# Chunk-sum tables of a state-space block: summing two products by accumulating matmuls instead of an elementwise add

## Chip, cores and metric

The kernel runs on one core of a Trainium2 chip. The metric is the time of one execution on the device, in microseconds (us). TensorE, VectorE, ScalarE, GpSimd and the DMA queues each work through an instruction list of their own, in order; semaphores join them. In the rows, PE is TensorE's matmuls, PEld its weight loads, DVE VectorE, ACT ScalarE, POOL GpSimd.

## The reference

Two transformer-like blocks follow one another on a 512 x 1024 sequence. Only the first block is touched: one layer of latent attention beside a two-directional diagonal state-space mixer.

```python
h = _rms_norm(x, pre_norm_g[l])
z = h @ w_in[l]
z_q, z_kv, z_kr, g_attn, u_ssm, g_ssm = jnp.split(z, split_points, axis=-1)
attn = _mla_attention(z_q, z_kv, z_kr, positions, ...)
...
lam_bar = jnp.exp(lam * dt)
b_bar = ((lam_bar - 1.0) / lam)[..., None] * b
bu = jnp.einsum('sbgh,gph->sbgp', u_c, b_bar)          # complex
_, h = lax.associative_scan(_diag_scan_op, (a, bu), reverse=reverse, axis=0)
y = y + jnp.real(jnp.einsum('sbgp,ghp->sbgh', h, c))
```

There are 32 groups of 16 channels, 64 complex states per group and two directions (2 x 64 = 128 partitions).

## The kernel before

The scan is done in 64 chunks of 8 positions. For each group a table F holds lam_bar to a power (1 to 8) times b_bar, real and imaginary part; F transposed, times the chunk's inputs `U`, is the chunk's sum. A recurrence over the chunks (`recur`, with `step` and the `fx` corrections) then runs on VectorE in the tile `st`.

The 32 groups go in 8 slices of 4. `table` makes a slice's table on VectorE with three passes over 128 x 1024 elements: a product into `tb` (line 457), a product into `ot` (line 457), and their sum into `tb` (line 458). `f_slice` then transposes the table on TensorE, 8 transposes per slice into PSUM tiles `ftr` (line 474); ScalarE copies each bank of four to an SBUF tile `f` (line 476); 8 matmuls of `f` with `U` write `vps` (line 481), each recorded as two passes in the trace; ScalarE copies `vps` to `st` in two halves (line 483). `rounds` staggers the slices: in one round a slice is multiplied, the next one transposed, and the one after that gets its table.

`table` is also used by `prep` for another set of tables (EP, EQ times c): two of these come ahead of the recurrence, six later.

Work around it, on the same engines: the projection to `U`; two gate projections of 96 matmuls each, the first (i = 0) free to run, the second (i = 1) ordered on TensorE behind the last chunk-sum matmul; then the projection `z` and its norm (`zn`, `ztr`, `zl`), the products V and QR made from it, and after these the attention heads, which are interleaved with the remaining tables and the outputs `y_slice`. The order of each engine's list is set when the program is built, from a timeline of estimated durations; the chip then runs each list in order.

Buffers by tag that matter here: "E" 2 (`tb`), "et" 1 (`ot`), "PT" 4 (`f` among others), "Y" 1 (the later `yo`). PSUM banks: two each for "tr", "sc", "o", "mm".

Of the kernel before, what the change touches and what calls it, by code (L numbers as in the profile page):

```python
# [64 lines left out]
class Net:  # L65
# [240 lines left out]
    def block1(self):  # L306

        nc, A, tc = self.nc, self.A, self.tc
        mm = nc.tensor.matmul
# [7 lines left out]
        for o in ORD1.split():  # L317
            n = int(o[1])
# [4 lines left out]
            elif o[0] == "g":  # L323
                g = self.gain("pre_norm_g", 0, tag="E")
# [31 lines left out]
        def feat(wh, wl, m):  # L356
            p = self.ps("mm")
            ms = slice(m * 128, (m + 1) * 128)
            for k in range(8):
                self.mm3(self.tiled(p), wh[k][:, ms], wl[k][:, ms], xh[k], xl[k], k == 0, k == 7)  # L360
            return p

        def tok(wh, wl, t, cw):
            p = self.ps("mm")
            for k in range(8):
                self.mm3(p[:, :cw], xh[k][:, t], xl[k][:, t], wh[k], wl[k], k == 0, k == 7)
            return p[:, :cw]
# [4 lines left out]
        for t in range(NT):  # L372
            p = tok(wh, wl, t, 512).rearrange("p (g h) -> p g h", g=G)
            nc.scalar.copy(yt[:, :, 2 * t], p[0:64])
            nc.scalar.copy(yt[:, :, 2 * t + 1], p[64:128])
        U = self.act(shape=[128, G, 64], name="U", tag="U")
        for q in range(4):
            p = self.ps("tr" if q < 2 else "sc", "utr")
# [47 lines left out]
        br, bi = bB[:, 0], bB[:, 1]  # L426
        braw = [self.act(shape=[128, G, 16], name="braw", tag="S") for _ in range(2)]
        for i in range(2):
# [6 lines left out]
        EP, EQ, FP, FQ = (self.act(shape=[128, G, 2, 8], name=n, tag=t)  # L435
                          for n, t in (("EP", "sq"), ("EQ", "sq"), ("FP", "T"), ("FQ", "T")))
# [11 lines left out]
        nc.scalar.copy(EQ[:, :, 0], EP[:, :, 1])  # L448
        nc.scalar.activation(EQ[:, :, 1], EP[:, :, 0], AF.Copy, scale=-1.0)

        def table(P, Q, xr, xi, s):

            sh = [128, 4, 16, 16]
            o, t = (self.act(shape=sh, name=n, tag=g) for n, g in (("tb", "E"), ("ot", "et")))
            for d, p, x in ((o, P, xr), (t, Q, xi)):
                p = p[:, s * 4:s * 4 + 4].rearrange("p g r e -> p g (r e)")[:, :, :, None].to_broadcast(sh)
                nc.vector.tensor_tensor(d, p, x[:, :, None, :].to_broadcast(sh), OP.mult)
            nc.vector.tensor_tensor(o, o, t, OP.add)
            return o.rearrange("p g (r e) h -> p g r (e h)", r=2)

# [3 lines left out]
        last = [None]  # L464

        def f_slice(s):
            gs = slice(s * 4, s * 4 + 4)
            ft = table(FP, FQ, br[:, gs], bi[:, gs], s)
            yield
            f = []  # L470
            for r in range(2):
                p = self.ps("sc" if s % 2 else "tr", "ftr")
                for gg in range(4):
                    nc.tensor.transpose(p[:, gg * 128:(gg + 1) * 128], ft[:, gg, r], self.ident)
                f.append(self.act(shape=[128, 4, 128], name="f", tag="PT"))
                nc.scalar.copy(f[r].rearrange("p g e -> p (g e)"), p)
            yield
            pv = self.ps("o", "vps").rearrange("p (g r c) -> p g r c", r=2, g=4)
            for r in range(2):
                for gg in range(4):  # L480
                    last[0] = mm(pv[:, gg, r], f[r][:, gg], U[:, s * 4 + gg], start=True, stop=True)
            for ps_, o in ((slice(0, 64), 1), (slice(64, 128), -1)):
                nc.scalar.copy(st[ps_, gs].rearrange("p g r j s -> p (g r) j s"),
                               pv[ps_, :, :, ::o].rearrange("p g r (s j) -> p (g r) j s", j=8))

        rounds((s, f_slice(s)) for s in range(8))


# [47 lines left out]
        def prep(s):  # L536

            gs = slice(s * 4, s * 4 + 4)
            c_ = self.small([128, 2, 4, 16], bufs=2, name="cc")
            for i in range(2):  # L540
                nc.sync.dma_start(c_[:, i], A["s5_c"][i][:, gs])
            e = table(EP, EQ, c_[:, 0], c_[:, 1], s)
            nc.sync.dma_start(Ed[s], e.rearrange("p g r e -> p (g r e)"))
            yield
            bb = bbs[s % 2]
            for d in range(2):
                ps_, cs_ = slice(d * 64, d * 64 + 64), slice(d * 32, d * 32 + 16)
                nc.scalar.copy(bb[ps_, :, :, cs_], bB[ps_, :, gs])
            p = self.ps("sc", "kps")
            for gg in range(4):  # L550
                for r in range(2):
                    mm(p[:48, gg * 128:(gg + 1) * 128], bb[:, r, gg], e[:, gg, r], start=r == 0, stop=r == 1)
            kst = self.act(shape=[128, 4, 8, 16], name="kst", tag="K")
            pv = p.rearrange("p (g t h) -> p g t h", g=4, t=8)
            nc.scalar.copy(kst[0:48], pv[0:48])
            k7 = self.small([16, 4, 16], bufs=1, name="k7")
            nc.scalar.copy(k7, pv[32:48, :, 7])
            dd = self.small([16, 4, 16], bufs=1, name="dd")
            nc.vector.tensor_tensor(dd, Dd[:, gs, None].to_broadcast([16, 4, 16]),
                                    self.ident[0:16, None, 0:16].to_broadcast([16, 4, 16]), OP.mult)  # L560
            nc.vector.tensor_tensor(k7, k7, dd, OP.add)
            nc.vector.tensor_tensor(kst[0:16, :, 0], kst[0:16, :, 0], k7, OP.add)
            kd = Kd[s]
            nc.sync.dma_start(kd[:, :, 112:240], kst[0:16].rearrange("p g t h -> p g (t h)"))
            nc.sync.dma_start(kd[:, :, 0:112], kst[32:48, :, 0:7].rearrange("p g t h -> p g (t h)"))
# [51 lines left out]
        for i in range(2):  # L617
            wh, wl = self.weights([A["w1_in"][1 + i, j] for j in range(4)])
            for m in range(4):
                with ExitStack() as late:  # L620
                    if i:
                        late.enter_context(tc.issue_after(last[0].ins))
                    p = feat(wh, wl, m)
# [49 lines left out]
        for t in range(NT):  # L673
            ts = slice(t * 128, (t + 1) * 128)
            p = self.ps("mm")
            self.mm3(p, Z[0][:, 2, ts], Z[1][:, 2, ts], wk_h[1], wk_l[1], True, True)
            self.split(V[0][:, t], V[1][:, t], p)
        for t in range(NT):
            ts = slice(t * 128, (t + 1) * 128)
            p = self.ps("mm")  # L680
# [3 lines left out]
            pv = p[:, :256].rearrange("p (h f) -> p h f", h=4)  # L684
            pv, qav, qbv = (a.rearrange("p h (a f) -> p h a f", a=2) for a in (pv, qa, qb))
# [6 lines left out]
            p = self.ps("tr", "qtr")  # L692
# [97 lines left out]
        def rnorm(i):  # L790
            p = self.ps("g", "nps")
            for t in range(NT):
                mm(p[:, 2 * t:2 * t + 2], sqa[i][:, t * 128:(t + 1) * 128], ones, start=True, stop=True)
            s_ = self.small([128, NT], name="nss", bufs=2)
            nc.vector.tensor_copy(s_, p[:, 0:8].rearrange("p (t a) -> p t a", a=2)[:, :, 0])
            return self.rowsum(s_, 512)

        y = [self.b8([128, 4, 512], F32, name="y1") for _ in range(2)]
        r = rnorm(0)
        for half in range(2):  # L800
            wh, wl = self.weights([A["w1_out"][half, i] for i in range(2)])
            for t in range(NT):
                p = self.ps("g", "mm")
# [8 lines left out]
        sh, sl = (self.b8([128, 4, 512], name=n) for n in ("sgh", "sgl"))  # L812
# [4 lines left out]
        for m in range(4):  # L817
            p = self.ps("g", "mm")
# [7 lines left out]
            f = self.act(name="gf", tag="c")  # L826
# [3 lines left out]
        r = rnorm(1)  # L830
        mark = self.last_y
        g = self.gain("post_norm_g", 0, mark, "E")
# [5 lines left out]
        for t in range(NT):  # L838
            ss = self.small([128, 2], name="pss")
            gy = []  # L840
            for half in range(2):
                wh, wl = w[half]
                p = self.ps("g", "mm")
# [705 lines left out]
```

## Time and profile before

| | before |
|---|---|
| median of 3 runs | 1656.55 us |
| lowest, highest run | 1652.34, 1658.28 us |
| the profiled execution | 1654.3 us |
| span of its instructions | 1652.0 us |
| granted TensorE clock, mean | 0.983 |
| TensorE busy in the span | 96% |
| VectorE busy in the span | 58% |
| ScalarE busy in the span | 48% |

The profiled execution is 2.25 us below the median; 2.3 us of it lie outside the span. Shares of the whole span are means over the stages of two blocks, so the stretch around the change has to be looked at by itself: the chunk sums stand between 43 and 92 us of the span, the recurrence and the projections behind them up to about 172 us.

### The profile page before, as it was taken

The numbers are of one execution on the slowest core, as the hardware profiler recorded it, in microseconds if no ns is written. First come the engines' busy times: TensorE is split into PE (matmuls) and PEld (weight loads), VectorE is DVE, ScalarE is ACT, GpSimd is POOL, SyncE is SP. The second block draws the span as 40 slices with busy tenths as digits, with TensorE's granted clock in tenths as the row PEclk, the third lists the DMA queues.
The fourth block names the chain that finished last, engine by engine and source line by source line (L and its number), as shares of the span: only waits on it lengthen the run. The fifth ranks groups of instructions, "written<-read, shape, count | busy, mean of one in ns | idle before, by whom it ended". The sixth has DMA issues, their size and how long they took to land.

```text
span 1652.0 us, 22681 instructions
## 1 busy us (share of the span) xinstructions
PE 1591.1 (96%) x8240; PEld 1342.2 (81%) x8240; DVE 952.2 (58%) x1863; ACT 794.7 (48%) x1548; POOL 397.7 (24%) x492
## 2 busy tenths in 40 slices
PE   7997999899999999999999999999999999999998
PEld 5876888688888888888888888888878888888886
DVE  7989665855787865323333465488865632333334
ACT  5734686543677845333232443377774433323242
POOL 2001120413465712101010130355571210101012
PEclk9987999999999999999999999999999999999999
DMA  4222343444222442333333333412233233333332
GB/s 163 85 77 70 110 118 122 160 151 154 54 63 57 116 153 77 97 89 96 102 102 102 103 130 118 149 48 56 58 101 128 64 99 93 102 103 102 102 100 79
DMA packets 71406, 167.43 MB, mean 101 GB/s; under 512 B 14464, under 2 KB 23168, under 8 KB 71296
## 3 DMA queue, kind: packets, MB, share of 16 engines
q1 hardware_dynamic: 70528, 165.21, 32.7%
q8 instruction: 65, 1.06, 0.3%
q10 hardware_dynamic: 768, 0.79, 0.2%
q14 instruction: 45, 0.37, 0.1%
HBM read 145.80 MB, written 10.98 MB: 95 GB/s over the span
## 4 chain that ended last, share of the span: by engine, by line
PE 72%; issue 10%; DVE 9%; ACT 4%; DMA 2%; POOL 2%; ACTq 0%; SPq 0%; DVEq 0%; POOLq 0%
PE mm L177 20%; PE mm L175 20%; PE mm L176 20%; PE ptr L953 2%; DVE sc L928 2%; DVE pt L145 1%; PE cps L1001 1%; PE oacc L963 1%; PE oacc L962 1%; PE sc L927 1%; PE sc L924 1%; DMA ql<-ql 1%; ACT ysq L207 1%; DMA swap<-raw 1%; DVE wlo L145 1%
## 5 line engine op out<-in xcount | busy, mean ns | idle before, releaser
L145 DVE TENSOR_TENSOR wlo<-wst,whi 128x1024 fp32r<-128x1024 f32 (+3 forms) x209 | 254.7, 1223 | 252.9 <-ACT whi L144 249.1
L175 PE MATMUL mm<-xT,whi 128*128 128x512 f32 (+1 forms) x896 | 338.3, 381 | 0.1
L144 ACT CAST whi<-wst 128x1024 fp32r<-128x1024 f32 (+3 forms) x209 | 215.1, 1033 | 253.8 <-PE mm L177 125.1
L176 PE MATMUL mm<-xT,whi 128*128 128x512 f32 (+1 forms) x896 | 335.8, 376 | 0.0
L177 PE MATMUL mm<-xT,wlo 128*128 128x512 f32 (+1 forms) x896 | 326.7, 377 | 0.9 <-DVE wlo L145 0.8
L1389 POOL TENSOR_TENSOR relu<-relu 128x512 f32<-128x512 f32 x64 | 67.0, 1046 | 539.7 <-ACT relu L1388 539.7
L177 PE MATMUL mm<-whi,hl 128*128 128x512 f32 x512 | 195.9, 389 | 0.0
L176 PE MATMUL mm<-wlo,hh 128*128 128x512 f32 x512 | 195.9, 389 | 0.0
L177 PEld LDWEIGHTS mm<-xT,wlo 128*128 128x128 f32 x896 | 169.0, 189 | 32.3 <-DVE wlo L145 1.8
L176 PEld LDWEIGHTS mm<-xT,whi 128*128 128x128 f32 x896 | 169.1, 189 | 27.5
L175 PEld LDWEIGHTS mm<-xT,whi 128*128 128x128 f32 x896 | 168.6, 189 | 27.9 <-ACT xT L144 0.4
L175 PE MATMUL mm<-whi,hh 128*128 128x512 f32 x512 | 188.2, 389 | 0.0
L931 ACT ACTIVATE sc<-sc,mn 128x512 f32<-128x512 f32 x192 | 107.1, 559 | 31.1 <-DVE mn L928 23.1
L145 DVE TENSOR_TENSOR hl<-relu,hh 128x512 fp32r<-128x512 f32 x64 | 51.9, 810 | 119.4 <-ACT hh L144 117.2
L145 DVE TENSOR_TENSOR pt<-ptr,pt 128x256 fp32r<-128x256 f32 (+1 forms) x160 | 95.4, 605 | 38.5 <-ACT pt L144 37.6
L176 PEld LDWEIGHTS mm<-wlo,hh 128*128 128x128 f32 x512 | 96.1, 188 | 20.0
L177 PEld LDWEIGHTS mm<-whi,hl 128*128 128x128 f32 x512 | 96.1, 188 | 20.0
L175 PEld LDWEIGHTS mm<-whi,hh 128*128 128x128 f32 x512 | 96.1, 188 | 19.9
L1388 ACT ACTIVATE relu<-mm 128x512 f32<-128x512 f32 x64 | 38.4, 600 | 148.3 <-PE mm L177 148.3
L928 DVE CUSTOM_DVE_ANT_0 sc<-sc,c_mask 128x512 f32<-128x512 f32 x192 | 87.2, 483 | 30.9 <-PE sc L927 29.9
L144 ACT CAST pt<-ptr 128x256 fp32r<-128x256 f32 (+1 forms) x160 | 81.4, 516 | 43.1 <-PE ptr L953 38.6
L940 POOL TENSOR_SCALAR sc<-sc,smx,gt 128x512 f32<-128x512 f32 (+3 forms) x128 | 79.0, 628 | 75.0 <-DVE smx L935 58.6
(394 smaller groups left out, 2956.0 us busy)
## 6 DMA issues: line engine op xcount, KB each, us to landing
wst<-in_w_up_t SPq DMA_DIRECT2D x64, 512.0 KB
wst<-in_w_down_t SPq DMA_DIRECT2D x64, 512.0 KB
wst<-in_w_in_m SPq DMA_DIRECT2D x24, 512.0 KB
wst<-in_w_in_a SPq DMA_DIRECT2D x16, 512.0 KB
x<-x SPq DMA_DIRECT2D x32, 256.0 KB
w<-in_cw SPq DMA_DIRECT2D x32, 256.0 KB
wst<-in_w_out_t SPq DMA_DIRECT2D x16, 512.0 KB
wst<-in_w_in SPq DMA_DIRECT2D x8, 512.0 KB
```

The costliest lines, as they stand in the source:

```text
L144: self.nc.scalar.copy(hi, src)
L145: self.nc.vector.tensor_tensor(lo, src, hi.bitcast(F32), OP.subtract)
L175: mm(ps, lh, rh, start=first, stop=False)
L176: mm(ps, lh, rl, start=False, stop=False)
L177: mm(ps, ll, rh, start=False, stop=last)
L207: self.nc.scalar.activation(self.act(name="ysq", tag="PT"), y, AF.Square, scale=D ** -0.5, accum_out=ss)
L928: nc.vector.tensor_tensor_reduce(out=sreg[i], in0=p, in1=self.mask[:, 512 - w:512], scale=1.0, scalar=3e38, op0=OP.add, op1=OP.min, accum_ ...
L931: self.mark = nc.scalar.activation(sreg[i], sreg[i], AF.Exp, bias=mn[:, i:i + 1], scale=-1.0, accum_out=sm[:, i:i + 1])
L940: nc.gpsimd.tensor_scalar(sreg[i], sreg[i], sm[:, i:i + 1], rgate[:, i:i + 1], OP.mult, OP.mult)
L953: self.pe = nc.tensor.transpose(p[:, c:c + 128], sreg[i][:, j * 128:(j + 1) * 128], self.ident)
L1388: nc.scalar.activation(a, p, AF.Relu)
L1389: nc.gpsimd.tensor_tensor(a, a, a, OP.mult)
```

## The change

`table` gets a switch. For the chunk sums the sum of the two products is left out; both products are returned, each is transposed and copied by itself, and each product's matmul accumulates into the same PSUM region. The second product of even slices gets the "Y" buffer, of odd slices the "et" buffer. The `prep` tables keep the add.

```diff
-        def table(P, Q, xr, xi, s):
+        def table(P, Q, xr, xi, s, add=True):
...
-            o, t = (self.act(shape=sh, name=n, tag=g) for n, g in (("tb", "E"), ("ot", "et")))
+            o, t = (self.act(shape=sh, name=n, tag=g)
+                    for n, g in (("tb", "E"), ("ot", "et" if add or s % 2 else "Y")))
...
+            if not add:
+                return [a.rearrange("p g (r e) h -> p g r (e h)", r=2) for a in (o, t)]
             nc.vector.tensor_tensor(o, o, t, OP.add)
...
-            ft = table(FP, FQ, br[:, gs], bi[:, gs], s)
+            fts = table(FP, FQ, br[:, gs], bi[:, gs], s, False)
             yield
             f = []
-            for r in range(2):
-                p = self.ps("sc" if s % 2 else "tr", "ftr")
-                for gg in range(4):
-                    nc.tensor.transpose(p[:, gg * 128:(gg + 1) * 128], ft[:, gg, r], self.ident)
-                f.append(self.act(shape=[128, 4, 128], name="f", tag="PT"))
-                nc.scalar.copy(f[r].rearrange("p g e -> p (g e)"), p)
+            for i, ft in enumerate(fts):
+                for r in range(2):
+                    p = self.ps("sc" if i else "tr", "ftr")
+                    for gg in range(4):
+                        nc.tensor.transpose(p[:, gg * 128:(gg + 1) * 128], ft[:, gg, r], self.ident)
+                    f.append(self.act(shape=[128, 4, 128], name="f", tag="PT"))
+                    nc.scalar.copy(f[-1].rearrange("p g e -> p (g e)"), p)
...
-                    last[0] = mm(pv[:, gg, r], f[r][:, gg], U[:, s * 4 + gg], start=True, stop=True)
+                    mm(pv[:, gg, r], f[r][:, gg], U[:, s * 4 + gg], start=True, stop=False)
+                    last[0] = mm(pv[:, gg, r], f[2 + r][:, gg], U[:, s * 4 + gg], start=False, stop=True)
```

## Rows read from the trace of the kernel before

**Rows 1.** The page's first part: busy time, share, instructions of each engine.

```profile
PE 1591.1 (96%) x8240; PEld 1342.2 (81%) x8240; DVE 952.2 (58%) x1863; ACT 794.7 (48%) x1548; POOL 397.7 (24%) x492
```

**Rows 2.** Busy time by stretches: length, engines' busy us, granted clock, DMA.

```profile
54.00:84.00 30.00, 29.63 (x217) 27.38 (x215) 29.05 (x39) 21.91 (x38) 0.00 (x0) 1.00 0.17 52
84.00:90.20 6.20, 5.24 (x24) 4.96 (x25) 5.33 (x5) 2.00 (x4) 0.00 (x0) 0.58 0.42 120
90.20:95.40 5.20, 5.20 (x15) 4.09 (x15) 5.06 (x8) 1.16 (x2) 0.00 (x0) 0.52 0.57 214
95.40:142.00 46.60, 45.50 (x223) 37.47 (x222) 40.73 (x86) 15.96 (x36) 3.29 (x6) 1.00 0.19 51
142.00:146.00 4.00, 1.84 (x9) 0.87 (x7) 4.00 (x7) 2.40 (x7) 1.76 (x2) 1.00 0.59 182
146.00:172.00 26.00, 19.88 (x63) 13.93 (x63) 24.40 (x42) 11.41 (x18) 0.00 (x0) 0.54 0.22 79
172.00:200.00 28.00, 28.00 (x189) 23.96 (x188) 17.47 (x40) 16.88 (x37) 5.05 (x6) 1.00 0.32 87
```

**Rows 3.** VectorE's groups between 43 and 91.8 us: count, busy, mean.

```profile
L458 DVE TENSOR_TENSOR tb<-tb,ot 128x1024 f32<-128x1024 f32 x10 | 12.2, 1222 | 0.0
L457 DVE TENSOR_TENSOR ot<-FQ,bbar 128x1024 f32<-128x1024 f32 x8 | 9.8, 1222 | 0.0
```

**Rows 4.** Timeline of VectorE: start, length.

```profile
46.77 1.22 DVE L457 TENSOR_TENSOR ot<-FQ,bbar 128x1024 f32<-128x1024 f32 x1
...
49.14 1.22 DVE L458 TENSOR_TENSOR tb<-tb,ot 128x1024 f32<-128x1024 f32 x1
...
83.68 1.23 DVE L458 TENSOR_TENSOR tb<-tb,ot 128x1024 f32<-128x1024 f32 x1
...
91.77 0.68 DVE L501 TENSOR_TENSOR rt<-PA,st 128x512 f32<-128x512 f32 x1
```

**Rows 5.** Timeline of TensorE's matmuls.

```profile
54.01 1.91 PE L474 MATMUL ftr<-c_ident,tb 128*128 128x128 f32 x16
55.68 0.47 PE L175 MATMUL mm<-xT,whi 128*128 128x512 f32 x1
...
60.34 3.68 PE L481 MATMUL vps<-U,f 128*128 128x64 f32 x32
63.86 1.04 PE L474 MATMUL ftr<-c_ident,tb 128*128 128x128 f32 x8
...
84.96 1.97 PE L474 MATMUL ftr<-c_ident,tb 128*128 128x128 f32 x8 [1.33 <-DVE tb L458]
86.81 3.68 PE L481 MATMUL vps<-U,f 128*128 128x64 f32 x16
90.24 0.77 PE L175 MATMUL mm<-xT,whi 128*128 128x512 f32 x1
...
142.06 0.39 PE L175 MATMUL mm<-whi,zh 128*128 128x512 f32 x1
```

**Rows 6.** Timeline of ScalarE.

```profile
47.68 1.57 ACT L382 COPY U<-utr 128x512 f32<-128x512 f32 x3
...
55.41 2.07 ACT L476 COPY f<-ftr 128x512 f32<-128x512 f32 x4
...
64.06 1.18 ACT L483 COPY st<-vps 64x512 f32<-64x512 f32 x2 [0.61 <-PE vps L481]
...
90.52 1.17 ACT L483 COPY st<-vps 64x512 f32<-64x512 f32 x2 [2.91 <-PE vps L481]
```

**Rows 7.** VectorE's groups between 142 and 172 us.

```profile
L521 DVE TENSOR_TENSOR st<-st,fx 128x784 f32<-128x784 f32 x5 | 4.9, 972 | 0.0
L520 DVE TENSOR_TENSOR fx<-st,PA 128x784 f32<-128x784 f32 x5 | 4.9, 970 | 0.0
L457 DVE TENSOR_TENSOR ot<-EQ,cc 128x1024 f32<-128x1024 f32 x3 | 3.7, 1228 | 0.0
...
L458 DVE TENSOR_TENSOR tb<-tb,ot 128x1024 f32<-128x1024 f32 x2 | 2.5, 1226 | 0.0
```

## Prediction

> **What bounds the kernel now.** I began with the busy shares of the page. TensorE is busy 96% of the span and VectorE 58% [rows 1], which says that on the whole the matmuls are the limit, and nothing about the 50 us that the change touches. So I cut the stretch from 54 to 200 us into pieces and read the busy times of each [rows 2].
>
> Between 54 and 84 us, where the chunk sums are made, two engines are full at once: VectorE 29.05 of 30 us, TensorE 29.63 of 30 at a granted clock of 1.00. ScalarE has 8 us free. From 95.4 to 142 us TensorE is again full (45.50 of 46.60), VectorE has a few free microseconds (40.73 of 46.60). From 142 to 172 us TensorE is starved: busy 1.84 of 4 and 19.88 of 26, the latter at a clock of 0.54 (the lower of the two levels for most of it), while VectorE works 28.40 of 30 us. From 172 us on TensorE is full at clock 1.00, 28.00 of 28. So whatever moves the moment now at 172 us moves the end by as much; up to there VectorE and TensorE hand the lead to each other.
>
> The timelines show how the hand-over goes. VectorE ends the last chunk-sum table at 83.68 + 1.23 = 84.91 us [rows 4]; TensorE has waited 1.33 us for it, transposes it, and does the last 16 passes from 86.81 to 90.49 [rows 5]; ScalarE's copies to `st` end at 91.69 [rows 6]; VectorE starts the recurrence at 91.77 [rows 4]. The second gate's matmuls, kept behind the last chunk-sum matmul by the code, start at 90.24; after them come z and, at 142.06, the first product made from z [rows 5]. Two chains therefore leave the chunk sums: the recurrence on VectorE, and gate, z, V, QR on TensorE. Both meet before the heads at 172 us.
>
> **The change, part by part.**
>
> *VectorE.* Eight adds go, 1.222 us each [rows 3] (the other two of the ten there belong to `prep`): −9.8 us. That counts only where VectorE ends last.
>
> *TensorE.* Transposes go from 64 to 128. Sixteen of them took from 54.01 to 55.68 [rows 5], 0.104 us each; 64 more are +6.7 us. Matmuls go from 64 to 128, in the trace from 128 to 256 passes. Thirty-two passes took from 60.34 to 63.86 [rows 5], 0.110 each; 128 more are +14.1 us. Together +20.8 us on an engine that has only 0.37 us free in the 30 us where they stand [rows 2]. Whether the second, accumulating matmul into the same region costs more than the first is not to be seen by itself, but the two passes of one matmul already add into one region, so I price it as a pass: between 0.104, the quickest of the neighbouring rows, and 0.115 (3.68 over 32), which moves the term by under 1 us.
>
> *ScalarE.* Sixteen more copies; four took 2.07 us [rows 6], 0.52 each: +8.3 us. ScalarE has 8.1 us free in 54 to 84 and more behind it [rows 2], so the sum is covered. If the cover is gone, each copy delays the matmuls that wait for it, which is counted in the next part.
>
> *Buffers.* A slice now fills all four "PT" tiles, two slices did before. The copies of slice s+1 wait for slice s's matmuls, and the `st` copies of slice s stand in ScalarE's list beside them. After the last matmul of a slice TensorE can do what is left of the next one's transposes (some 0.8 us, half of 16 x 0.104) while ScalarE does two `f` copies (1.04) and perhaps the two `st` copies (1.18) [rows 6]. The hole is 0.2 to 1.4 us; with the waits between engines, 0.04 us in [rows 5, 6] (64.02 to 64.06) and more where four of them follow one another, I take 1.2 us for each of seven slice changes, 8.4 us. First-gate matmuls fill these holes, so they are not lost to TensorE, but they push the chunk sums back. What "Y" does for even slices is to leave VectorE free to run ahead; its price is nothing, because VectorE has become the quicker side (two products, 2.44 us, for a slice [rows 3], against TensorE's 5.2 us below).
>
> *Where the chunk sums now end.* A slice costs TensorE 16 x 0.104 + 32 x 0.110 = 5.2 us, eight 41.4. The first table is ready with its second product, at 46.77 + 1.22 = 48.0 us [rows 4], and `U` at 49.25 [rows 6]. If nothing came between: 48.0 + 41.4 + about 1 us for the first copies = 90.5 us, the same as now. If all first-gate matmuls still come between: 90.5 + 20.8, less what TensorE lost between 54 and 90.2 us, that is 1.3 us idle and 5.24 x 0.42 = 2.2 us by the clock [rows 2]: 108 us. My value, with the holes: 90.5 + 8.4 = 99 us, so the recurrence starts about 8.5 us late.
>
> *From there to 172 us.* The VectorE chain has the same work as before behind 91.77 us and hardly any gaps to close (40.73 of 46.60, then 28.40 of 30 [rows 2]): +8.5 us. The TensorE chain has 20.8 us more and gets back the idle 1.3 us and the clock losses of 84 to 95.4 us, 2.2 + 2.5 [rows 2], if TensorE stays busy there: z ends 14.8 us late. In the 30 us after z, though, 16.0 of VectorE's 28.4 us are recurrence corrections and `prep` tables [rows 7], and as these are only 8.5 us late, up to 6.3 us of them are out of the way when z arrives. So the two chains give +8.5 to +14.8 us; I take +10, near the lower end, since VectorE's load is what fills the stretch.
>
> The sum against the profiled execution: 1654.3 + 10 = 1664.3 us. That execution lies 2.25 us below the median, so the median goes from 1656.55 to about 1666.5. The added matmuls that a count over the whole span would put in TensorE's 4% of idle time do not find it there: of the 20.8 us most are paid.
>
> **Rivals.**
>
> *A. VectorE alone sets the time up to 172 us, and TensorE's extra work goes into its slack.* For it: VectorE is full in every stretch up to 172 us except 95.4 to 142, and TensorE is starved after 142. The eight adds would give −9.8 us. Against it: TensorE's slack from 54 to 172 us is 0.37 + 0.96 + 1.10 + 2.16 + 6.12 = 10.7 us idle and 2.2 + 2.5 + 19.88 x 0.46 = 13.8 us by the clock [rows 2], 24.5 in all, of which 20.8 would be used up. So no more than −3.7 us is open unless work changes its place across 172 us, and that only if every gap closes. It decides if the chunk sums end before about 82 us, which the 41.4 us from 48.0 do not allow. Time 1647 (all of it) to 1653. Chance 0.10. The Trainium skill (Perfetto Trace Analysis, Identifying the Most-Contended Engine) ranks VectorE by its occupancy and TensorE by the share of weight loads, and has the most-contended one optimized first; by that rule 29.05 against 27.38 of 30 us [rows 2] makes VectorE the one, and the time would be 1656.55 − 9.8 = 1646.8.
>
> *B. The chunk sums win every hole.* If the built order puts them ahead of the first gate, they end at 91 to 94 us, the recurrence is 0 to 3 us late, z 14.8 us late, and the stretch after z shrinks from 30 to some 20 us, because VectorE's 16.0 us [rows 7] are then mostly done. The 172 us moment moves by 0 to +5: 1656.5 to 1661.5. The present order speaks against it: between 55.68 and 60.34 us TensorE ran first-gate matmuls [rows 5] although the copies they stood in front of ended at 57.48 [rows 6]. Chance 0.22.
>
> *C. The four "PT" buffers turn each slice into a round trip, and TensorE drops to the lower clock once the gate's matmuls are used up.* The place is the second half of the chunk sums; it decides when a hole has nothing to fill it. The row for it: after the 1.33 us wait at 84.96 us sixteen passes took 3.68 us, as long as thirty-two at clock 1.00 [rows 5]; the stretch had a clock of 0.58 [rows 2]. Two slices at that pace add 2 x 5.2 = 10.4 us to my +10: about 1677; with unfilled holes of 1.4 us in four slices 1682. Against it: more work per slice on TensorE makes holes smaller in proportion. Chance 0.18.
>
> **How the numbers follow.** My forecast (+6 to +15) has the remaining chance, 0.50. About 0.5% is what a measurement of this kernel can tell from no change: 8.3 us, that is below 1648.3 or above 1664.8. My forecast lies above that bound in 0.34 of its 0.50, C always; A ends below it in 0.06 of its 0.10. Slower 0.52, same 0.42, faster 0.06. The range leaves out the better half of A and the far end of C: 1653 to 1680. The forecast's own range is 1662 to 1672.
>
> **What would show it.** Right: the last chunk-sum matmul near 99 us instead of 90.5, VectorE with some 15 us of gaps before the recurrence, the clock at 1.00 from 54 to 142 us, z's end near 157 us, and the heads starting near 182 instead of 172 us. For A the heads would start before 172; for B the last chunk-sum pass would lie below 94 us with first-gate matmuls behind it; for C the clock column would show well under 1.00 between 80 and 105 us. The prediction is wrong if the stretch after 172 us absorbs or enlarges the shift, or if a pass in an accumulating pair takes much over 0.11 us.

## The result

The changed kernel took 1668.86 us in the median of 4 runs (1667.12 to 1671.61) against 1656.92 for the kernel before (1652.34 to 1658.28, 4 runs): 11.9 us between the medians, a ratio of 1.0092 with a 95% interval of 1.0072 to 1.0111. The ratio stands for 15.2 us (11.9 to 18.4), the medians for the lower end of that. The profiled execution took 1667.22 us with a span of 1665.3, 13.3 us longer than before. The forecast was 1666.5 us, in a range of 1653 to 1680, slower by 10 us.

The same stretches as in [rows 2], in the changed kernel (length, then busy us of TensorE's matmuls and loads, VectorE, ScalarE, GpSimd; granted clock; DMA share and GB/s):

```profile
54.00:84.00 30.00, 30.00 (x218) 27.78 (x216) 15.96 (x23) 16.87 (x28) 0.00 (x0) 1.00 0.07 19
84.00:90.20 6.20, 5.62 (x51) 5.30 (x50) 3.01 (x3) 5.00 (x9) 0.00 (x0) 1.00 0.46 157
90.20:95.40 5.20, 5.20 (x51) 5.20 (x50) 3.03 (x4) 3.64 (x7) 0.00 (x0) 1.00 0.30 88
95.40:142.00 46.60, 46.60 (x277) 39.99 (x276) 36.06 (x56) 18.78 (x34) 0.00 (x0) 1.00 0.23 70
142.00:146.00 4.00, 2.98 (x15) 2.26 (x14) 3.49 (x17) 1.58 (x8) 1.87 (x4) 1.00 0.32 56
146.00:172.00 26.00, 20.33 (x88) 15.67 (x87) 24.85 (x50) 12.89 (x23) 3.13 (x4) 0.83 0.25 73
172.00:200.00 28.00, 25.19 (x128) 19.78 (x129) 22.85 (x45) 12.88 (x29) 2.08 (x3) 0.80 0.20 69
```

From 54 to 84 us VectorE has fallen from 29.05 to 15.96 us of work, and TensorE has not a gap left. From 84 to 142 us TensorE lacks 0.58 us, and the clock is 1.00 where it was 0.58 and 0.52. The starved stretch at a low clock has moved behind 157 us; up to 200 us TensorE is not yet full as it was from 172 on.

TensorE's timeline in the changed kernel: one slice (its second product transposed at 58.80, its first matmul at 59.68, its first accumulating matmul, of line 488, at 64.62), then the last first-gate matmul, the last chunk-sum passes, the first product made from z, and the first score of the heads. Behind it stand ScalarE's copies of that slice's second product:

```profile
58.80 1.05 PE L479 MATMUL ftr<-c_ident,ot 128*128 128x128 f32 x8
59.68 0.33 PE L487 MATMUL vps<-U,f 128*128 128x64 f32 x2
59.85 1.04 PE L479 MATMUL ftr<-c_ident,tb 128*128 128x128 f32 x8
60.65 0.47 PE L177 MATMUL mm<-xT,wlo 128*128 128x512 f32 x1
...
64.39 0.40 PE L175 MATMUL mm<-xT,whi 128*128 128x512 f32 x1
64.62 0.33 PE L488 MATMUL vps<-U,f 128*128 128x64 f32 x2
...
87.96 0.48 PE L177 MATMUL mm<-xT,wlo 128*128 128x512 f32 x1
...
106.97 0.39 PE L488 MATMUL vps<-U,f 128*128 128x64 f32 x2
...
156.84 0.48 PE L175 MATMUL mm<-whi,zh 128*128 128x512 f32 x1
...
186.13 0.63 PE L175 MATMUL sc<-qkh 128*128 128x512 f32 x2
```

```profile
60.20 1.08 ACT L481 COPY f<-ftr 128x512 f32<-128x512 f32 x2
```

The last passes start at 106.97 us, where those of before ended at 90.49; the first product made from z starts at 156.84 instead of 142.06 [rows 5]; the heads start at 186.13, before at 172.81. The slice's copies end at 61.28 us, yet its accumulating matmuls wait until 64.62 behind seventeen first-gate matmuls that the built list has put in front of them. The last first-gate matmul starts at 87.96, so the whole first gate is done before nearly all matmuls of the last four slices.

VectorE's groups between 43 and 105 us (count, busy, mean, and the idle time ahead of them with its releaser), and the start of the recurrence:

```profile
L459 DVE TENSOR_TENSOR ot<-FQ,bbar 128x1024 f32<-128x1024 f32 x8 | 9.7, 1223 | 15.1 <-PE ftr L479 15.1
...
L459 DVE TENSOR_TENSOR tb<-EP,cc 128x1024 f32<-128x1024 f32 x2 | 2.4, 1222 | 3.9 <-PE ftr L479 3.9
L459 DVE TENSOR_TENSOR ot<-EQ,cc 128x1024 f32<-128x1024 f32 x1 | 1.2, 1224 | 2.9 <-PE ftr L479 2.9
```

```profile
108.74 0.69 DVE L508 TENSOR_TENSOR rt<-PA,st 128x512 f32<-128x512 f32 x1
```

The adds are gone, and in their place VectorE waits 15.1 + 3.9 + 2.9 = 21.9 us for TensorE's transposes to give its table buffers back (the prediction had some 15). The recurrence starts 17.0 us later than at 91.77 [rows 4].

### The profile page after: what moved, and what is told of

The parts are those of the page before. It is cut to its first block, busy times and chain, and to the rows that moved or that the text cites. A ratio compares the mean times of both kernels' runs of the same rounds, so it can differ in the third digit from the quotient of the medians.

```text
span 1665.3 us, 23094 instructions
## 1 busy us (share of the span) xinstructions
PE 1605.5 (96%) x8432; PEld 1358.3 (82%) x8432; DVE 942.9 (57%) x1855; ACT 804.8 (48%) x1564; POOL 397.9 (24%) x492
## 4 chain that ended last, share of the span: by engine, by line
PE 76%; DVE 9%; issue 5%; ACT 5%; DMA 2%; POOL 2%; ACTq 0%; SPq 0%; DVEq 0%; POOLq 0%
PE mm L175 21%; PE mm L177 21%; PE mm L176 21%; PE ptr L960 2%; DVE sc L935 2%; DVE pt L145 1%; DMA swap<-raw 1%; ACT sc L938 1%; PE vps L488 1%; PE vps L487 1%; PE cps L1008 1%; PE ftr L479 1%; PE oacc L970 1%; PE kps L559 1%; PE sc L934 1%
## 5 line engine op out<-in xcount | busy, mean ns | idle before, releaser
L938 ACT ACTIVATE sc<-sc,mn 128x512 f32<-128x512 f32 x192 | 107.1, 559 | 30.7 <-DVE mn L935 23.2
```

The source lines that it names most:

```text
L938: self.mark = nc.scalar.activation(sreg[i], sreg[i], AF.Exp, bias=mn[:, i:i + 1], scale=-1.0, accum_out=sm[:, i:i + 1])
```

## The experiments

Three theories were held against each other. Theory 1: TensorE's added work sets the time, and the adds' removal is worth little. Theory 2: the late recurrence sets it. Theory 3: the adds' 9.8 us are gained in full, and a larger TensorE cost hides them. Ratios are to the kernel before, run on the same chip as the kernel in question; a thousandth is 1.65 us. "Recurrence", "z" and "heads" are the starts, in the profiled execution, of the first recurrence step, the first product made from z, and the first score.

| kernel | ratio (95% interval) | recurrence | z | heads |
|---|---|---|---|---|
| before | 1 | 91.77 | 142.06 | 172.81 |
| changed | 1.0092 (1.0072 to 1.0111) | 108.74 | 156.84 | 186.13 |
| changed, gates behind | 1.0113 (1.0098 to 1.0127) | 92.68 | 168.59 | 187.26 |
| changed, adds kept | 1.0101 (1.0079 to 1.0122) | 109.22 | 157.33 | 186.64 |
| before, adds left out | 0.9992 (0.9979 to 1.0004) | 89.78 | 138.09 | 169.32 |
| changed, two sets of f | 1.0079 (1.0063 to 1.0094) | 110.12 | 158.25 | 189.18 |
| before, adds on GpSimd | 1.0096 (1.0072 to 1.0121) | 104.20 | 156.34 | 188.25 |
| change in odd slices | 1.0110 (1.0085 to 1.0135) | 109.35 | 160.05 | 193.09 |
| transposes alone | 1.0034 (1.0018 to 1.0049) | 96.07 | 147.31 | 176.73 |
| before, matmuls doubled | 1.0068 (1.0047 to 1.0088) | 103.02 | 151.81 | 183.11 |
| before, gates behind | 1.0080 (1.0053 to 1.0106) | 91.91 | 169.29 | 189.87 |
| before, fewer matmuls | 0.9992 (0.9975 to 1.0008) | 91.16 | 141.33 | 170.18 |
| the same, adds left out | 0.9943 (0.9924 to 0.9961) | 81.26 | 128.75 | 160.94 |

**Both gates behind the chunk sums.**

```diff
-                    if i:
+                    if True:
                         late.enter_context(tc.issue_after(last[0].ins))
```

> The changed kernel, with both gate projections (not only the second) kept behind the last chunk-sum matmul on TensorE. Theory 1, TensorE's added work sets the time: the sum of its work is the same, so z ends at 156.8 us or later, by as much as the holes between slices now stay empty (up to some 10 us), and the time is 1667 to 1678. Theory 2, the late start of the recurrence (108.7 us in the changed kernel against 91.8 before) sets it: the chunk sums end near 49 + 41.4 + 8 = 98 to 100 us, the recurrence starts 7 to 9 us earlier, and the time falls to 1660 to 1662.

The ratio is 1.0113, no better than the changed kernel's. The recurrence starts 16 us earlier than there, at 92.68; z comes 11.8 us later, the heads 1.1. A row of busy times for the eight slices of this kernel:

```profile
47.20:91.00 43.80, 43.71 (x383) 43.35 (x384) 26.32 (x39) 27.52 (x51) 0.00 (x0) 0.96 0.09 28
```

TensorE lacks 0.09 us in 43.80, with the same four "PT" tiles: the buffers and the copies make no hole between slices, and a slice takes 5.5 us, near the 5.2 worked out. The fall in time that theory 2 forecast does not come, although the recurrence is early by more than it asked for. The early recurrence does give something behind z: the stretch from z to the heads shrinks from 29.3 to 18.7 us. It is paid back because z comes later, and not through holes between the slices, as the expectation of theory 1 had it. Two stretches of this kernel show where TensorE lost the time:

```profile
43.00:54.00 11.00, 10.04 (x78) 9.86 (x79) 10.97 (x19) 9.16 (x18) 0.00 (x0) 0.69 0.37 116
142.00:157.00 15.00, 10.72 (x50) 8.73 (x49) 11.99 (x20) 8.12 (x14) 2.35 (x4) 0.99 0.26 84
```

Without first-gate matmuls to do, it works 10.04 of 11 us at a clock of 0.69 around the first tables, where the changed kernel works 11.00 at 1.00; and between 142 and 157 us it works 10.72 of 15, the changed kernel 13.98. So this kernel has the recurrence early and z late, and does not say what an early recurrence would be worth with z where it was.

**The adds kept.**

```diff
             if not add:
+                nc.vector.tensor_tensor(o, o, t, OP.add)
                 return [a.rearrange("p g (r e) h -> p g r (e h)", r=2) for a in (o, t)]
```

> The changed kernel with the add put back into the first product's tile, while both tiles are still transposed, copied and multiplied (so the second product counts twice in the sums): VectorE's work as before the change, TensorE's and ScalarE's as after it. Theory 1 (TensorE's work is the cost, the add's removal is worth little because VectorE now waits 15 us for transposes): 1668 to 1673, that is 0 to 4 us above the changed kernel. Theory 3 (the adds' 9.8 us are gained in full and hide part of a larger TensorE cost): 1677 to 1680.

The ratio is 1.0101, within the interval of the changed kernel, and the heads start 0.5 us later. With TensorE's chunk-sum work doubled, eight adds more or less are not seen. Theory 3 falls: its 1677 to 1680 us would be a ratio of 1.014 or more, outside the interval.

**The adds left out, TensorE as before.**

```diff
-            nc.vector.tensor_tensor(o, o, t, OP.add)
+            if add:
+                nc.vector.tensor_tensor(o, o, t, OP.add)
...
-            ft = table(FP, FQ, br[:, gs], bi[:, gs], s)
+            ft = table(FP, FQ, br[:, gs], bi[:, gs], s, False)
```

> The kernel before, with the eight adds left out and nothing put in their place: both products are still made on VectorE, only the first is transposed and multiplied (the second product is missing from the chunk sums). TensorE's and ScalarE's work as before, VectorE 9.8 us less. Theory 1: TensorE is full from 54 to 84 us anyway, VectorE is ahead by itself only from 84 to 95 and from 142 to 172 us, so 3 to 8 us of the 9.8 are gained: 1649 to 1654. Theory 3: all of it, 1647. If the adds were covered by TensorE altogether: 1656 to 1658.

The ratio is 0.9992: −1.3 us, between −3.5 and +0.7, less than the 3 to 8 that were expected. In the profile the heads start 3.5 us earlier. So the work that the change takes away was nearly free even before anything is added to TensorE.

**Two sets of transposed tables.**

```diff
-                    f.append(self.act(shape=[128, 4, 128], name="f", tag="PT"))
+                    f.append(self.act(shape=[128, 4, 128], name="f", tag="S" if s % 2 else "PT"))
```

> The changed kernel, with the transposed tables of odd slices in the six S buffers instead of the four PT buffers, so that two slices' tables fit as before the change. Theory 1: the gate matmuls between the slices stand there by the built order, TensorE loses nothing in them, so the chunk sums may end a little earlier but z does not: 1666 to 1670. Rival C of the prediction (the four buffers make each slice a round trip): the chunk sums end 6 to 9 us earlier and the time falls to 1660 to 1663.

The ratio is 1.0079; the interval overlaps the changed kernel's, and the recurrence starts 1.4 us later, not 6 to 9 earlier. With the first experiment this takes the four buffers out of the question for the changed kernel.

**The adds on GpSimd.**

```diff
-            nc.vector.tensor_tensor(o, o, t, OP.add)
+            (eng or nc.vector).tensor_tensor(o, o, t, OP.add)
...
-            ft = table(FP, FQ, br[:, gs], bi[:, gs], s)
+            ft = table(FP, FQ, br[:, gs], bi[:, gs], s, nc.gpsimd)
```

> The kernel before, with the eight adds of the chunk-sum tables on GpSimd, which is idle there; everything else as before. Theory 1 (TensorE's work sets the time; the adds alone are worth 0 to 3.5 us, as the kernel without them showed): 0.998 to 1.001 of the time before, since TensorE keeps its load, and GpSimd's 2.6 to 3.6 us for an add (twice its 1.31 to 1.80 us for 128x512 elements) may delay a slice. Theory 3 (VectorE's 9.8 us count): 0.994. If GpSimd's slower add becomes the pace of the slices: 1.002 or more.

The ratio is 1.0096, as slow as the change, and the third case of the expectation. GpSimd's group and VectorE's table groups in that kernel, and single operations of the two engines:

```profile
L458 POOL TENSOR_TENSOR tb<-tb,ot 128x1024 f32<-128x1024 f32 x8 | 22.7, 2844 | 46.0 <-DVE ot L457 35.0 <-DVE tb L457 11.0
```

```profile
L457 DVE TENSOR_TENSOR tb<-FP,bbar 128x1024 f32<-128x1024 f32 x8 | 14.5, 1822 | 1.6 <-PE ftr L474 1.6
L457 DVE TENSOR_TENSOR ot<-FQ,bbar 128x1024 f32<-128x1024 f32 x8 | 9.7, 1215 | 2.3 <-POOL tb L458 2.3
```

```profile
53.75 2.44 POOL L458 TENSOR_TENSOR tb<-tb,ot 128x1024 f32<-128x1024 f32 x1 [2.25 <-DVE ot L457]
...
66.42 2.72 POOL L458 TENSOR_TENSOR tb<-tb,ot 128x1024 f32<-128x1024 f32 x1 [2.54 <-DVE tb L457]
```

```profile
53.73 0.22 DVE L303 TENSOR_TENSOR cm<-PA 128x64 f32<-128x64 f32 x1
53.98 2.30 DVE L304 TENSOR_TENSOR PA<-cm,cm 128x64 f32<-128x64 f32 x1
...
66.79 3.42 DVE L457 TENSOR_TENSOR tb<-FP,bbar 128x1024 f32<-128x1024 f32 x1
```

An add takes 2.84 us on GpSimd, and VectorE operations that start during one are held: the 128x64 operation at 53.98 takes 2.30 us, where its neighbour takes 0.22, and ends at 56.28 when the add ends at 56.19; the table product at 66.79 takes 3.42, where its group took 1.22 before. TensorE then waits for tables: it is busy for 25.26 us of 30 from 54 to 84, at a clock of 0.93, and from 84 to 107 us its clock is 0.50. The Trainium skill (Perfetto Trace Analysis, Optimizing Scalar/DVE Operations) warns that VectorE and GpSimd share a read port of SBUF, so that moving work between them might not help; these rows agree.

**The change in every second slice.**

```diff
-            fts = table(FP, FQ, br[:, gs], bi[:, gs], s, False)
+            two = s % 2 == 1
+            fts = table(FP, FQ, br[:, gs], bi[:, gs], s, not two)
+            fts = fts if two else [fts]
...
+                    last[0] = mm(pv[:, gg, r], f[r][:, gg], U[:, s * 4 + gg], start=True, stop=not two)
+                    if two:
+                        last[0] = mm(pv[:, gg, r], f[2 + r][:, gg], U[:, s * 4 + gg], start=False, stop=True)
```

> The change in the four odd slices only: 10.4 us more on TensorE, 4.9 us less on VectorE. Theory 1: TensorE's extra work is paid less what idle and slow-clock time between 84 and 95 us gives back (up to 6 us, once): 4 to 7 us slower, 1.003 to 1.004. If the cost came with the accumulation into one region or with a fixed disturbance of the order, it would be the full 1.008 to 1.009.

The ratio is 1.0110: half the added work cost as much as all of it, which theory 1 had not expected. Busy times of that kernel:

```profile
84.00:95.00 11.00, 9.57 (x74) 9.20 (x74) 4.81 (x4) 5.39 (x10) 0.00 (x0) 0.89 0.01 2
95.00:107.00 12.00, 10.25 (x69) 9.60 (x69) 7.17 (x6) 4.60 (x9) 0.00 (x0) 0.78 0.35 115
```

TensorE lacks 1.43 and 1.75 us here and runs at clocks of 0.89 and 0.78, where the changed kernel lacks 0.58 and is at 1.00. It waits for `f` copies (3.9 us in five waits between 60 and 108 us). These are the signs of rival C of the prediction, holes with nothing to fill them and a lower clock, in a kernel in which they were not looked for. Why the waits are longer than in the changed kernel was not tried further.

**Transposes alone, and matmuls alone.** The first is the changed kernel with the matmuls of the first product only, the second the kernel before with each matmul done twice.

```diff
-                    mm(pv[:, gg, r], f[r][:, gg], U[:, s * 4 + gg], start=True, stop=False)
-                    last[0] = mm(pv[:, gg, r], f[2 + r][:, gg], U[:, s * 4 + gg], start=False, stop=True)
+                    last[0] = mm(pv[:, gg, r], f[r][:, gg], U[:, s * 4 + gg], start=True, stop=True)
```

> The changed kernel without the accumulating matmuls: both products are transposed and copied, the matmuls read the first alone (the second product is missing from the sums). TensorE has 6.7 us more than before. If the extra work is paid in proportion (12 of 20.8 us): +4 us, 1.002 to 1.003. If the idle and slow-clock time is used first: 0 to +1, 0.999 to 1.001. If the copies on ScalarE and the four full buffers were the cost: the full 1.008.

```diff
-                    last[0] = mm(pv[:, gg, r], f[r][:, gg], U[:, s * 4 + gg], start=True, stop=True)
+                    mm(pv[:, gg, r], f[r][:, gg], U[:, s * 4 + gg], start=True, stop=False)
+                    last[0] = mm(pv[:, gg, r], f[r][:, gg], U[:, s * 4 + gg], start=False, stop=True)
```

> The kernel before, with each chunk-sum matmul done twice into the same region, and the adds kept (the sums come out doubled). TensorE has 14.1 us more, no transpose and no copy is added. In proportion: +8 us, 1.005. If idle and slow-clock time is used first: +8 as well, at most 14 (1.008) if VectorE's adds then delay it in addition. If accumulating were free because of pipelining: 1.000.

The 6.7 us of transposes cost 0.34% (5.6 us, 3.0 to 8.1), the 14.1 us of passes 0.68% (11.2, 7.8 to 14.6). All 20.8 cost 0.92% (15.2, 11.9 to 18.4). That is 0.84, 0.79 and 0.73 of the work added: within the intervals the cost goes with the work, and no first portion is free. The kernel with transposes alone also has all the added copies and fills all four "PT" tiles; as its interval ends at 1.0049, these are not the 1.008 that the change costs. The accumulating matmuls are neither free nor dearer than the first ones, as the changed kernel's two groups of passes show, first and accumulating:

```profile
L487 PE MATMUL vps<-U,f 128*128 128x64 f32 x119 | 22.7, 271 | 0.0
L488 PE MATMUL vps<-U,f 128*128 128x64 f32 x118 | 22.4, 272 | 0.6 <-ACT f L481 0.6
```

**The kernel before with both gates behind.** The same edit as in the first experiment, on the kernel before.

> The kernel before, with both gate projections behind the last chunk-sum matmul. Nothing is added; the first gate's 96 matmuls (some 17 us of them stood between the slices) no longer fill TensorE's waits for VectorE's tables, 3.7 us a slice against 2.6 us of TensorE work. Theory 1: some 8 us of waits stay empty, the clock may drop there, and z comes later by as much: 4 to 15 us slower, 1.003 to 1.009. If the order of the first gate is of no matter: 0.999 to 1.001; if the earlier recurrence counts: below 0.998.

The ratio is 1.0080. The recurrence starts when it did (91.91 against 91.77 us), z 27 us later.

```profile
54.00:84.00 30.00, 28.34 (x154) 26.91 (x155) 24.60 (x35) 13.79 (x25) 0.00 (x0) 0.61 0.00 1
```

From 54 to 84 us TensorE is busy for 28.34 us at a clock of 0.61; before it was 29.63 at 1.00 [rows 2]. The first gate had filled TensorE's waits for VectorE's tables (with 11.3 us of matmuls between the slices from 54 us on, not the 17 of the expectation). In this order, where TensorE has room, the change itself costs less: 1.0113 against 1.0080, 0.3% where it is 0.9% in the other order.

**Fewer chunk-sum matmuls, with and without the adds.**

```diff
-            for r in range(2):
-                for gg in range(4):
-                    last[0] = mm(pv[:, gg, r], f[r][:, gg], U[:, s * 4 + gg], start=True, stop=True)
+            for gg in range(4):
+                g0 = min(s * 4 + gg, 30)
+                last[0] = mm(pv[:, gg].rearrange("p r c -> p (r c)"), f[gg % 2][:, gg],
+                             U[:, g0:g0 + 2].rearrange("p g c -> p (g c)"), start=True, stop=True)
```

> The kernel before with half as many chunk-sum matmuls: four of 128 columns in place of eight of 64 in each slice, each with one of the two transposed tables (so the sums are not those of the reference); adds, transposes and copies stay. TensorE has about 6 us less (64 passes fewer at 0.110, the others a little longer), VectorE as before. Theory 1, taken to its end (TensorE's total sets this stage before the change too): 3 to 5 us faster, 0.997 to 0.998. If VectorE holds the stage as soon as TensorE has less: no change, 0.999 to 1.001.

> The same with the eight adds left out as well (and so the second product): TensorE about 6 us less, VectorE 9.8 us less. If the two engines tie in the kernel before, so that relief of one alone is lost on the other: 5 to 8 us faster, 0.995 to 0.997, more than the sum of the two single kernels. If TensorE alone sets it: as the kernel with fewer matmuls alone.

Eight passes of 128 columns took from 67.03 to 67.92 us, 0.111 each, no longer than those of 64; so TensorE has 64 x 0.11 = 7 us less, and not 6. TensorE's relief alone gives 0.9992. The adds left out alone gave 0.9992. Both give 0.9943, that is −9.4 us (−12.6 to −6.4), where the two single gains add up to −2.6. Busy times from 54 to 84 us, first with fewer matmuls alone, then with the adds left out as well:

```profile
54.00:84.00 30.00, 26.25 (x153) 22.28 (x152) 28.52 (x37) 21.24 (x36) 0.00 (x0) 0.91 0.23 67
```

```profile
54.00:84.00 30.00, 30.00 (x190) 26.45 (x189) 27.72 (x40) 23.09 (x39) 0.00 (x0) 1.00 0.28 88
```

Relieved alone, TensorE waits (26.25 of 30, clock 0.91) for a VectorE that stays full; with VectorE relieved too it is full again, and the recurrence starts 10 us earlier, the heads 12. The two engines tie in the kernel before. None of the kernels that compute the reference's result was faster than the kernel before.

## Why the prediction was right, and where it was off

**What bounds the stage: right.** That VectorE and TensorE are both full from 54 to 84 us was the reading on which all rested. The tie is shown: relieving VectorE alone or TensorE alone gains 1.3 us, both together 9.4.

**TensorE's +20.8 us: right.** In the changed kernel eight transposes take 0.80 us to the next instruction (59.85 to 60.65), 0.100 each against 0.104, and the two passes of a matmul take 0.22 us to the next matmul (64.79 to 65.01 in the same timeline), first and accumulating ones alike. z was forecast 14.8 us late, by the added work less the idle and slow-clock time given back; it came 14.8 us late (156.84 against 142.06), at a clock of 1.00 from 54 to 142 us, as said.

**The step that failed: "I take 1.2 us for each of seven slice changes, 8.4 us".** It put the end of the chunk sums at 99 us; they end near 107.4, at the far bound of 108. The hole between slices is not made by the buffers and the copies: with the gates moved behind, TensorE lacks 0.09 us over all eight slices, and a second set of tiles does not help. In the changed kernel itself the last slices, behind the first gate, have the same four tiles and no hole: TensorE is busy for all of 90.20 to 142 us. The delay is made by the built list, which puts 3.97 us of first-gate matmuls (60.65 to 64.62) into a slice whose copies are done at 61.28, and in the end the whole first gate ahead of nearly all matmuls of the last four slices. That is the case that the bound of 108 us was worked out for. The term should have been 16.9 us in place of 8.4. z did not move by it, since TensorE works through the hole and the first-gate matmuls are due before z in any case; the recurrence did, by 8.5 us more than forecast. Why the list has the gate there was not followed.

**The last step, +10 out of +8.5 to +14.8: mis-sized, by 3.3 us against the span.** I expected up to 6.3 us of VectorE's corrections out of the way when z arrives. With the recurrence 17.0 us late instead of 8.5, they were not: from z to the heads it took 29.3 us after 30.7, a relief of 1.5. So the heads moved by 14.8 − 1.5 = 13.3 us, and so did the span. The same 13.3 us come out along VectorE: the recurrence is 17.0 us late, and from there to the heads it takes 77.4 us in place of 81.0, 3.7 less. VectorE works 73.6 of the 79 us from 107 to 186 (31.30, 14.32, 14.02 and 14.00 in four stretches), so the late recurrence holds the heads nearly as tightly as the late z. No run separates the two: both come from TensorE's added work, and where the first gate keeps its place they move together. That +10 lies so near the measured 11.9 to 15.2 is in part luck, since one of the two chains was 8.5 us off.

**The rivals.** A, VectorE alone: refuted; leaving the adds out gains 1.3 us (at most 3.5), and keeping them in the changed kernel costs nothing that can be measured. The slack count behind A's bound (24.5 us of idle and slow-clock time to take up 20.8) was of no use as a hiding place: only 6.0 us of it, between 54 and 95 us, were regained before z; the rest lies behind z, where TensorE waits for VectorE and cannot be given work that is due earlier. B, the chunk sums in front of everything, did not happen in the changed kernel. Forced by moving both gates behind, its mechanism is real (recurrence on time, 18.7 us from z to the heads where "some 20" was written), but z then came 26.5 us late, not 14.8, and the kernel was no faster. B with the first gate still at work around the first tables was not built. C, holes and a lower clock: not in the changed kernel, but in the one with the change in every second slice.

**Left open.** The spans and the heads differ by 13.3 us, the timed runs by 11.9 (medians) to 15.2 (ratio). Single executions of the kernel before lie 5.9 us apart and those of the changed one 4.5, so no cause is needed for that. In some other kernels the heads and the span of one and the same execution shift by different amounts (changed with two sets of f: heads +16.4 us, span +11.9), so stages behind the heads move too, by up to 4.5 us; this was not followed.

## What to carry to other kernels

Where two engines are full in the same stretch, work moved from one to the other costs most of what the receiver must do (here 0.73 of it), and the giver's saving is worth next to nothing: price the receiver, and test the tie by relieving each alone and both together. Idle time is slack only if it comes before the work that has to use it is due. To place a stage's end, read which other work the built order puts between its instructions; the dependences allow more than the list does.

## What the runs showed that was not expected

- An add of 128x1024 on GpSimd took 2.84 us and stretched VectorE operations that started beside it from 0.22 to 2.30 us and from 1.22 to 3.42; the group of eight first table products rose to a mean of 1.82 us.
- Half of the change cost as much as the whole (1.0110 and 1.0092): 10.4 us of added work, then waits and a clock of 0.78 to 0.89 in place of 1.00. Why was not tried.
- Removing 7 us from TensorE alone, and 9.8 from VectorE alone, gave 0.08% each; both together 0.57%.
